# The scatter of a pair of experts' outputs, one token tile behind each step of the next pair's products, moved into groups of four tiles on four PSUM banks

## The chip, the core and the metric

One core of a Trainium2 chip runs the whole program in one launch. The metric is the device time of one execution in microseconds; the median of three runs is used. The engines are named as in the profile: PE is the matrix engine (its weight loads are listed apart as PEld), DVE, ACT and POOL are the vector, scalar and general engines, SP issues the weight loads, and the DMA engines carry them out.

## The reference, cut to what matters

The model has two layers. Each layer mixes tokens (an RG-LRU block in layer 0, an mLSTM in layer 1) and then applies a hierarchical mixture of experts. Layer 0 has 768 tokens (512 latent and 256 context), layer 1 has 512. For each token the mixture picks one of 4 groups and the best 2 of that group's 8 experts, 32 experts in all. The part that the change touches is this:

```
h2  = modulate(rms_norm(x, g2), sh2, sc2)
eid, wts = two experts of the best group, softmax of the two * p_group
f[token] = sum over its two experts of wts * ((silu(h2 @ w_gate[e]) * (h2 @ w_up[e])) @ w_down[e])
x   = x + gt2 * f
```

Everything is float32. An expert's three matrices are 1024x512, 1024x512 and 512x1024, so 6.29 MB; the 32 experts of a layer are 201.3 MB, and all of them are read once per layer.

## The kernel before, in words

Experts are worked on in 16 pairs per layer (index p, `moe`, the loop at line 1539). A pair has 128 slots, 64 per expert (96 and 32 for p = 5 to 10 of layer 0), and each slot holds one routed token. Per pair the program does, in this order:

- **Gate and up products** (`gate_up`, L1252): 16 steps. In a step the two experts of the pair each multiply one 128-row slice of their tokens with a 128x512 slice of a weight. Steps 0 to 3 use the first half of the gate matrices, 4 to 7 the first half of the up matrices, 8 to 11 and 12 to 15 the second halves. The sums gather in the PSUM tiles `pg` and `pu`. After each step, a table `fill` (step number to list of functions) says what else is put into the program there: loads of later weights, and the scatter of the pair before.
- **Transposes** of the next pair's gathered tokens (`tokens_T`, L1207) and of the hidden activations (`hidden_T`, L1268), and the look-up of a later pair's slots (L1165).
- **Down products** (`down`, L1277) in two column halves c = 0 and 1, into the PSUM tiles `pd`. DVE weighs each half with the gate (L1231, in layer 0 also L1235 and L1236), ACT rounds it to `yh` (L1239) and POOL forms the remainder `yl` (L1240).
- **Scatter** (`scatter_tile`, L1210 to L1215): the 128 slot rows go back to their tokens as a product with a one-hot table `oht`. For a token tile t (128 tokens) and a column half c this is two 128x512 matmuls on PE, one of `yh` and one of `yl`, into one PSUM bank (L1213), and one DVE addition of that bank to the token rows `x` in SBUF (L1215; the rows are named `xc` for context and `xl` for latent tokens). Layer 0 has 12 such (t, c) tiles per pair, layer 1 has 8. The list `todo` carries them to the next pair's `gate_up`; those of the last pair come after `rest()`, in turn on two `psc` and two `pdn` banks.

PSUM has eight banks here: two for `pg` and `pu`, two for `pd` (pool `pdn`), two for transposes (`ptr`), and two for the scatter (`psc`, tile name `ps`). The order of the work on PE, DVE, ACT, POOL and SP is that of the program text, since `manual_schedule` holds all five; a buffer is handed out again when its last reader is done, by semaphores.

Before the change, the pair's tiles stand one behind each of the last steps: steps 4 to 15 in layer 0, 8 to 15 in layer 1. In the last pair of a layer they stand in three groups behind steps 3, 7 and 11. All of them go through the two `psc` banks.

Weights come in pieces of 128 partitions x 8 KB (1.05 MB), 12 pieces (12.58 MB) per pair, through a ring of 15 buffers in layer 0 and 19 in layer 1 (`Ring`). SP issues them in program order (L93; the halves of the last pair's down matrices at L90), two behind every fourth step and four behind the down products; a load waits until the PE products that read its buffer are done.

Pair p = 5 of layer 0 (`extra`) has a second set of slots for its first expert: `more_up` runs behind steps 3, 7, 11 and 15 and keeps a `pdn` bank through the whole of `gate_up`; `more_scatter` follows behind step 3 of p = 6, after a one-hot table made on DVE (L1195).

Of the kernel before, what the change touches and what calls it, by code (L numbers as in the profile page):

```python
# [37 lines left out]
NPAIR = NE // 2  # L38
# [7 lines left out]
class Ring:  # L46
# [18 lines left out]
    def load(self, n, eng=None):  # L65
        for _ in range(n):
            if self.done < len(self.order):
                self.piece(*self.order[self.done], eng or self.net.nc.sync)
# [34 lines left out]
class Net:  # L103
# [994 lines left out]
    def moe(self, l, x, NT, ring, rt, tail):  # L1098
# [6 lines left out]
        with ExitStack() as st:  # L1105
# [21 lines left out]
            pdn = st.enter_context(tc.tile_pool(name="pdn", bufs=2, space=PSUM))  # L1127
            ptr = st.enter_context(tc.tile_pool(name="ptr", bufs=2, space=PSUM))
            psc = st.enter_context(tc.tile_pool(name="psc", bufs=2, space=PSUM))
# [61 lines left out]
            def onehot(oht, r):  # L1191

                rt_ = w1.tile([P, NT], F32, name="rt_")
                V.tensor_scalar(rt_, self.tile0[:, 0:NT], r, -1.0, op0=OP.subtract, op1=OP.mult)
                V.tensor_tensor(oht.rearrange("p (t n) -> p t n", n=P),  # L1195
                                self.iota1.unsqueeze(1).to_broadcast([P, NT, P]),
                                rt_.unsqueeze(2).to_broadcast([P, NT, P]), OP.is_equal)
# [5 lines left out]
            def tokens_T(xg, xT, n=P):  # L1203
                for h in range(2):
                    pt = ptr.tile([P, 4, P], F32, name="tr")
                    for j in range(4):
                        nc.tensor.transpose(pt[:, j, :], xg[:, h * 512 + j:h * 512 + 512:4], self.ident)  # L1207
                    nc.scalar.activation(xT[:, 4 * h:4 * h + 4, :], pt[:, :, 0:n], AF.Copy)  # L1208

            def scatter_tile(t, h, lhsT, ys, psum=None):  # L1210
                ps = (psum or psc).tile([P, 512], F32, name="pd" if psum is pdn else "ps")
                for i, y in enumerate(ys):
                    nc.tensor.matmul(ps, lhsT, y, start=i == 0, stop=i == len(ys) - 1)  # L1213
                xs = x[off + t][:, h * 512:(h + 1) * 512]
                V.tensor_add(xs, xs, ps)  # L1215

            def gates(r):

                g = w1.tile([P, D], F32, name="xg")
                V.tensor_scalar(g, gt[:, 0, :], r[:, 1:2], None, op0=OP.mult)  # L1220
                V.scalar_tensor_tensor(g, gt[:, 1, :], r[:, 2:3], g, op0=OP.mult, op1=OP.add)
                return g
# [19 lines left out]
            def gate_up(p, xT, fill):  # L1242

                e = (2 * p, 2 * p + 1)
                step = 0
                pg = pgu.tile([P, F], F32, name="pg")
                pu = pgu.tile([P, F], F32, name="pu")
                for h in range(2):
                    for n, ps in (("gate", pg), ("up", pu)):
                        for j in range(4):  # L1250
                            for a, w, i in cols(p):
                                nc.tensor.matmul(ps[a:a + w, :], xT[:, 4 * h + j, a:a + w],  # L1252
                                                 pieces[n, e[i], h][:, j, :], start=h == 0 and j == 0,
                                                 stop=h == 1 and j == 3)
                            for f in fill.pop(step, ()):
                                f()
                            step += 1
                s = w1.tile([P, F], F32, name="sg")
                nc.scalar.activation(s, pg, AF.Silu)  # L1259
                V.tensor_mul(s, s, pu)  # L1260
                return s

            def hidden_T(s):
                hT = w1.tile([P, 4, P], F32, name="hT")
                for h in range(2):
                    pt = ptr.tile([P, 4, P], F32, name="tr")[:, 0:2, :]
                    for j in range(2):
                        nc.tensor.transpose(pt[:, j, :], s[:, 256 * h + j:256 * h + 256:2], self.ident)  # L1268
                    nc.scalar.activation(hT[:, 2 * h:2 * h + 2, :], pt, AF.Copy)  # L1269
                return hT  # L1270
# [15 lines left out]
            extra = FIRST if l == 0 else None  # L1286
# [8 lines left out]
            def more_prep(p):  # L1295
                slots(p, table_more(p), rm, idm, P)
                gather(idm, xgm)

            def more_up(p, ps, h, c):

                if h == 0 and c == 0:
                    tokens_T(xgm, xTm, CAP)
                for j in range(4):
                    for a in range(2):
                        nc.tensor.matmul(ps[64 * a:64 * a + 64, 256 * c:256 * c + 256], xTm[:, 4 * h + j, :],
                                         pieces[("gate", "up")[c], 2 * p, h][:, j, 256 * a:256 * a + 256],
                                         start=h == 0 and c == 0 and j == 0,
                                         stop=h == 1 and c == 1 and j == 3, skip_group_check=True)
                if h == 1 and c == 1:
                    nc.scalar.activation(sm, ps[:, 0:256], AF.Silu)  # L1310
                    V.tensor_mul(sm, sm, ps[:, 256:512])
# [28 lines left out]
            def prepare(p):  # L1340

                rr[p] = wk.tile([P, 4], F32, name="slotr", bufs=4)
                idx = wk.tile([P, 1], I32, name="idx")
                oh = table(p)

                def step():
                    slots(p, oh, rr[p], idx, caps(p)[0])
                    xgs[p] = w1.tile([P, D], F32, name="xg")
                    gather(idx, xgs[p])
                return step  # L1350
# [187 lines left out]
            todo, nxt = [], None  # L1538
            for p in range(NPAIR):
                fill = {}  # L1540
                if p == 0:
                    fill = {1: [fill_ranks], 3: [fill_gather], 6: [fill_first]}
                    nxt = lambda: first[2]()
                for i, f in enumerate(todo):
                    at = 16 - len(todo) + i if p + 1 < NPAIR else 3 + 4 * (3 * i // len(todo))
                    fill.setdefault(at, []).append(lambda f=f: scatter_tile(*f))
                both = None
                if p + 1 == NPAIR:
                    if l == 0:
                        both = gates(rr[p])  # L1550
                    if begin:
                        begin(w1)

                for k in range(4):
                    fill.setdefault(4 * k + 3, []).append(lambda: load(2))
                if p == extra:
                    pm = pdn.tile([P, 512], F32, name="pd")
                    for k in range(4):
                        fill.setdefault(4 * k + 3, []).append(lambda k=k: more_up(extra, pm, k // 2, k % 2))
                elif p - 1 == extra:  # L1560
                    fill.setdefault(3, []).append(more_scatter)
                s = gate_up(p, xT, fill)
                if p + 1 < NPAIR:
                    xT = w1.tile([P, KD, P], F32, name="xT")
                    tokens_T(xgs[p + 1], xT)
                if nxt:
                    nxt()
                hT = hidden_T(s)
                nxt = prepare(p + 3) if p + 3 < NPAIR else None
                if p + 1 == extra:  # L1570
                    more_prep(extra)
                if p == extra:
                    more_down(p)
                oht = w1.tile([P, NT * P], F32R, name="oht")
                onehot(oht, rr[p][:, 0:1])
                yh = w1.tile([P, 2, 512], F32R, name="yh")
                yl = w1.tile([P, 2, 512], F32R, name="yl")
                for c in range(2):
                    down(p, hT, c, yh, yl, rr[p], both)
                load(4)  # L1580
                todo = [(t, c, oht[:, t * P:(t + 1) * P], (yh[:, c, :], yl[:, c, :]))
                        for c in range(2) for t in range(NT)]
# [587 lines left out]
```

## Time and profile before

| | |
|---|---|
| median of 3 runs | 1930.48 us (1927.62 to 1940.3) |
| the profiled execution | 1943.99 us, its span 1942.0 us |
| PE busy | 1799.0 us (93%) |
| PEld busy | 1009.0 us (52%) |
| DVE busy | 959.3 us (49%) |
| ACT busy | 542.7 us (28%) |
| POOL busy | 387.7 us (20%) |
| L1213, matmuls of yh (310) and yl (310) | 154.1 and 123.5 us |
| L1213, weight loads for yh (310) | 58.5 us |
| L1215, additions to xl (252) and xc (64) | 172.4 and 43.7 us |

The profile cuts the span into 40 slices of 48.55 us. The pairs of layer 0 lie in slices 10 to 21, those of layer 1 in slices 30 to 40. A matmul's listed duration overlaps that of the next one, so what a piece of work costs PE is read from the distance between starts, not from the durations.

### The profile page before, as it was taken

To read this page: it belongs to the slowest core of one execution; us is meant where nothing else is said; L and a number is where in the kernel's file an instruction comes from. 1 tells how busy PE (TensorE), PEld (TensorE's weight loads), DVE (VectorE), ACT (ScalarE), POOL (GpSimd) and SP (SyncE) were. 2 spreads that over 40 slices of the span, in tenths; PEclk is the share of its full clock that TensorE was granted. 3 is DMA by queue.
4 is the path that set the end of the run, shared out by engine and by line. 5 is a ranking of instruction groups with operands and counts; after the bars stand their busy time and mean duration, and the time that the engine had idled before them with its cause. 6 is when DMAs were issued, how large, how long until landed. Compare 5 with 4: busy or idle time off the path is not lost. (4 is left out here: it accounts for less than half of the span.)

```text
span 1942.0 us, 26118 instructions
## 1 busy us (share of the span) xinstructions
PE 1799.0 (93%) x10181; PEld 1009.0 (52%) x10181; DVE 959.3 (49%) x1879; ACT 542.7 (28%) x1007; POOL 387.7 (20%) x300
## 2 busy tenths in 40 slices
PE   7999988897999999999987998999978999999996
PEld 5777775683333333333336898976743333333332
DVE  5577767465454454444455743155552333233334
ACT  5367776222111101111115421145321111111112
POOL 3443311501101000101015242121211111110101
PEclk9999989898999999999998998999988999999998
DMA  9645432547999789999932544200869999999993
GB/s 326 186 142 163 152 109 76 188 152 311 420 419 397 278 326 409 389 403 389 400 117 76 176 139 155 85 1 17 311 257 400 421 421 420 421 422 421 421 420 135
DMA packets 158244, 527.75 MB, mean 272 GB/s; under 512 B 15132, under 2 KB 92194, under 8 KB 109988
## 3 DMA queue, kind: packets, MB, share of 16 engines
q1 hardware_dynamic: 151348, 497.09, 66.5%
q0 software_dynamic: 6768, 28.93, 3.8%
q8 instruction: 82, 1.34, 0.3%
q14 instruction: 46, 0.38, 0.1%
HBM read 518.59 MB, written 7.39 MB: 271 GB/s over the span
## 5 line engine op out<-in xcount | busy, mean ns | idle before, releaser
L1215 DVE TENSOR_TENSOR xl<-xl,ps 128x512 f32<-128x512 f32 x252 | 172.4, 687 | 335.6 <-PE ps L1213 335.6
L1213 PEld LDWEIGHTS ps<-yh,oht 128*128 128x128 f32 x310 | 58.5, 189 | 248.8 <-DVE xl L1215 129.0
L1213 PE MATMUL ps<-yh,oht 128*128 128x512 f32 x310 | 154.1, 497 | 8.9 <-DVEq L1356 6.1
L1200 POOL DMA_INDIRECT xg<-h_rows,idx x32 | 36.7, 1146 | 628.8 <-DVE slot L1185 263.1
L1277 PE MATMUL pd<-wring,hT 128*64 128x512 f32 (+1 forms) x616 | 152.4, 611 | 3.0 <-ACT hT L1269 2.6
L1252 PE MATMUL pu<-wring,xT 128*64 128x512 f32 (+1 forms) x576 | 154.1, 606 | 0.0
L309 POOL TENSOR_TENSOR wlo<-ws,whi 128x1024 fp32r<-128x1024 f32 x41 | 114.8, 2809 | 120.9 <-ACT whi L306 119.4
L1252 PE MATMUL pg<-wring,xT 128*64 128x512 f32 (+1 forms) x576 | 136.9, 601 | 0.0
L1240 POOL TENSOR_TENSOR yl<-yw,yh 128x512 fp32r<-128x512 f32 x60 | 76.6, 1277 | 255.5 <-ACT yh L1239 255.5
L1213 PE MATMUL ps<-yl,oht 128*128 128x512 f32 x310 | 123.5, 398 | 0.0
L1259 ACT ACTIVATE sg<-pg 128x512 f32<-128x512 f32 x32 | 19.1, 597 | 367.6 <-PE pg L1252 367.6
L1685 PE MATMUL pa<-whi,hhi 128*128 128x256 f32 x352 | 104.3, 296 | 9.1 <-ACT v L1782 9.0
L1239 ACT ACTIVATE yh<-yw 128x512 fp32r<-128x512 f32 x64 | 40.3, 630 | 251.7 <-DVE yw L1236 127.9
L1231 DVE SCALAR_TENSOR_TENSOR yw<-pd,slotr,gt2b 128x512 f32<-128x512 f32 x62 | 46.5, 751 | 118.9 <-PE pd L1277 118.9
L1685 PE MATMUL pa<-whi,hlo 128*128 128x256 f32 x352 | 103.3, 293 | 0.0
L1685 PE MATMUL pa<-wlo,hhi 128*128 128x256 f32 x352 | 102.9, 292 | 0.0
L1252 PE MATMUL pu<-yt,xT 128*64 128x512 f32 (+1 forms) x408 | 101.7, 605 | 0.0
L1208 ACT ACTIVATE xT<-tr 128x512 f32<-128x512 f32 x64 | 35.1, 596 | 221.0 <-PE tr L1207 221.0
L1277 PE MATMUL pd<-yt,hT 128*64 128x512 f32 (+1 forms) x376 | 87.6, 599 | 1.5 <-ACT hT L1269 1.0
L1252 PE MATMUL pg<-yt,xT 128*64 128x512 f32 (+1 forms) x400 | 84.7, 599 | 0.0
L1215 DVE TENSOR_TENSOR xc<-xc,ps 128x512 f32<-128x512 f32 x64 | 43.7, 687 | 82.1 <-PE ps L1213 82.0
L1277 PEld LDWEIGHTS pd<-wring,hT 128*64 128x64 f32 (+1 forms) x616 | 44.3, 133 | 75.7 <-issue 69.6
(627 smaller groups left out, 3727.9 us busy)
## 6 DMA issues: line engine op xcount, KB each, us to landing
wring<-in_l_moe_w_gate_dram SPq DMA_DIRECT2D x62, 1024.0 KB
wring<-in_l_moe_w_up_dram SPq DMA_DIRECT2D x61, 1024.0 KB
wring<-in_l_moe_w_down_dram SPq DMA_DIRECT2D x59, 1024.0 KB
yt<-in_l_moe_w_up_dram SPq DMA_DIRECT2D x41, 1024.0 KB
ws<-in_l_ada_w_dram SPq DMA_DIRECT2D x40, 1024.0 KB
yt<-in_l_moe_w_gate_dram SPq DMA_DIRECT2D x39, 1024.0 KB
yt<-in_l_moe_w_down_dram SPq DMA_DIRECT2D x35, 1024.0 KB
ws<-in_l_moe_w_gate_dram SPq DMA_DIRECT2D x24, 1024.0 KB
```

The costliest lines, as they stand in the source:

```text
L309: eng_lo.tensor_sub(lo, x, hi.bitcast(F32))
L1200: nc.gpsimd.indirect_dma_start(out=xg, out_offset=None, in_=hd, in_offset=bass.IndirectOffsetOnAxis(ap=idx[:, 0:1], axis=0))
L1208: nc.scalar.activation(xT[:, 4 * h:4 * h + 4, :], pt[:, :, 0:n], AF.Copy)
L1213: nc.tensor.matmul(ps, lhsT, y, start=i == 0, stop=i == len(ys) - 1)
L1215: V.tensor_add(xs, xs, ps)
L1231: V.scalar_tensor_tensor(y[k], ps, r[:, 1:2], g[:, 0, :], op0=OP.mult, op1=OP.mult)
L1239: nc.scalar.activation(yh, y, AF.Copy)
L1240: eng.tensor_sub(yl, y, yh.bitcast(F32))
L1252: nc.tensor.matmul(ps[a:a + w, :], xT[:, 4 * h + j, a:a + w], pieces[n, e[i], h][:, j, :], start=h == 0 and j == 0, stop=h == 1 and j == 3)
L1259: nc.scalar.activation(s, pg, AF.Silu)
L1277: nc.tensor.matmul(pd[a:a + w, :], hT[:, 2 * h + j, a:a + w], ring.down(2 * p + i, h, j, c), start=h == 0 and j == 0, stop=h == 1 and j == 1)
L1685: nc.tensor.matmul(ps, h, w[:, k % 4, :], start=k == 0 and j == 0, stop=k == KD - 1 and j == 2)
```

## The change

Only the table of steps in the loop over pairs is written anew, and the choice of PSUM banks for a scatter tile.

```
+                n = 2 if p == extra else 4
                 for i, f in enumerate(todo):
-                    at = 16 - len(todo) + i if p + 1 < NPAIR else 3 + 4 * (3 * i // len(todo))
-                    fill.setdefault(at, []).append(lambda f=f: scatter_tile(*f))
+                    g, k = divmod(i, n)
+                    at = 15 * (g + 1) * n // len(todo) - (3 if p + 1 < NPAIR else 2) + (n == 2)
+                    fill.setdefault(at, []).append(lambda f=f, k=k: scatter_tile(*f, psum=(psc, pdn)[k // 2]))
```

The tiles now stand in groups of four: behind steps 2, 7 and 12 in layer 0, and behind steps 4 and 12 in layer 1; in the last pair of a layer behind 3, 8 and 13, and 5 and 13. The first two tiles of a group use the `psc` banks, the last two the `pdn` banks that the down products use between. In pair p = 5 of layer 0, where `more_up` holds one `pdn` bank, there are six groups of two behind steps 0, 3, 5, 8, 10 and 13, on `psc` alone. No instruction is added or removed; on ACT, POOL and SP nothing moves.

On PE, pair p = 2 of layer 0 (`pg`, `pu`: gate and up products; `xT`: the tokens; `ps`, `pd`: the banks), first the place where the first tile stood:

```order
L1252 MATMUL pg<-wring,xT 64x512 x8
L1252 MATMUL pu<-wring,xT 64x512 x2
L1213 MATMUL ps<-yh,oht 128x512
L1213 MATMUL ps<-yl,oht 128x512
L1252 MATMUL pu<-wring,xT 64x512 x2
```

(two matmuls of L1252 are one step), and now the end of step 2, the first group and the start of step 3, with the buffers' numbers, which tell the banks apart:

```order
L1252 MATMUL pg_4089<-wring_3777,xT_3966 64x512
L1252 MATMUL pg_4089<-wring_3789,xT_3966 64x512
L1213 MATMUL ps_4097<-yh_4027,oht_4023 128x512
L1213 MATMUL ps_4097<-yl_4028,oht_4023 128x512
L1213 MATMUL ps_4101<-yh_4027,oht_4023 128x512
L1213 MATMUL ps_4101<-yl_4028,oht_4023 128x512
L1213 MATMUL pd_4105<-yh_4027,oht_4023 128x512
L1213 MATMUL pd_4105<-yl_4028,oht_4023 128x512
L1213 MATMUL pd_4109<-yh_4027,oht_4023 128x512
L1213 MATMUL pd_4109<-yl_4028,oht_4023 128x512
L1252 MATMUL pg_4089<-wring_3777,xT_3966 64x512
L1252 MATMUL pg_4089<-wring_3789,xT_3966 64x512
```

The first tile moves from behind step 4 to behind step 2, and eight scatter matmuls now follow each other with no product between them.

On DVE, the start of pair p = 6 of layer 0, after the extra pair (`yw`: the weighed outputs of p = 5; `xc`, `xl`: additions of scatter tiles; L1194 and L1195: the table of `more_scatter`):

```order
L1236 TENSOR_TENSOR yw_5327<-yw_5327,sg_5329 128x512
L1215 TENSOR_TENSOR xc_2780<-xc_2780,ps_5376 128x512
L1215 TENSOR_TENSOR xc_2780<-xc_2780,ps_5380 128x512
L1215 TENSOR_TENSOR xl_2776<-xl_2776,pd_5384 128x512
L1215 TENSOR_TENSOR xl_2776<-xl_2776,pd_5388 128x512
L1194 TENSOR_SCALAR rt__5401<-tile0_82,rm_3677 128x6
L1195 TENSOR_TENSOR sg_5400<-iota1_58,rt__5401 128x768
```

Before, L1194 and L1195 came right behind L1236; now the four additions of the first group stand ahead of them.

## Rows read from the trace of the kernel before

**Rows 1.** The page: GB/s moved by DMA in each of the 40 slices.

```profile
GB/s 326 186 142 163 152 109 76 188 152 311 420 419 397 278 326 409 389 403 389 400 117 76 176 139 155 85 1 17 311 257 400 421 421 420 421 422 421 421 420 135
```

**Rows 2.** Timeline of PE, layer 0, p = 2: start, duration, instruction, count, idle.

```profile
518.27 3.60 PE L1252 MATMUL pg<-wring,xT 128*64 128x512 f32 x16
521.70 1.03 PE L1252 MATMUL pu<-wring,xT 128*64 128x512 f32 x4
522.66 0.50 PE L1213 MATMUL ps<-yh,oht 128*128 128x512 f32 x1
522.99 0.40 PE L1213 MATMUL ps<-yl,oht 128*128 128x512 f32 x1
523.32 1.08 PE L1252 MATMUL pu<-wring,xT 128*64 128x512 f32 x4
...
541.61 1.11 PE L1207 MATMUL tr<-ident,xg 128*128 128x128 f32 x8
...
551.43 3.60 PE L1252 MATMUL pg<-yt,xT 128*64 128x512 f32 x16
```

**Rows 3.** Timeline of PE, last scatter of layer 0, on four banks.

```profile
1014.78 0.39 PE L1213 MATMUL ps<-yl,oht 128*128 128x512 f32 x1
1015.01 0.40 PE L1213 MATMUL pd<-yh,oht 128*128 128x512 f32 x1
1015.24 0.39 PE L1213 MATMUL pd<-yl,oht 128*128 128x512 f32 x1
```

**Rows 4.** Timeline of PE, last pair of layer 1: a group of two tiles, then the end.

```profile
1904.40 0.64 PE L1252 MATMUL pg<-yt,xT 128*64 128x512 f32 x1
...
1907.98 0.50 PE L1213 MATMUL ps<-yh,oht 128*128 128x512 f32 x1
...
1909.11 3.65 PE L1252 MATMUL pu<-wring,xT 128*64 128x512 f32 x16
...
1918.14 3.60 PE L1277 MATMUL pd<-ws,hT 128*64 128x512 f32 x16
```

**Rows 5.** Timeline of PE, last pair of layer 0: third tile of a group.

```profile
984.87 0.50 PE L1213 MATMUL ps<-yh,oht 128*128 128x512 f32 x1 [1.45 <-DVE xc L1215]
```

**Rows 6.** Timeline of POOL, layer 0: the remainder of p = 1, c = 0.

```profile
518.06 1.27 POOL L1240 TENSOR_TENSOR yl<-yw,yh 128x512 fp32r<-128x512 f32 x1 [5.28 <-ACT yh L1239]
```

**Rows 7.** Timeline of DVE, layer 0: last read of the pd banks; table of more_scatter.

```profile
519.25 0.74 DVE L1235 SCALAR_TENSOR_TENSOR sg<-pd,slotr,gt2b 128x512 f32<-128x512 f32 x1
...
677.08 0.96 DVE L1195 TENSOR_TENSOR sg<-iota,rt__5385 128x768 fp32r<-128x768 f32 x1
```

**Rows 8.** Timeline of PE, layer 0: the two longest waits, before p = 5 and in p = 6.

```profile
613.76 0.32 PE L1165 MATMUL tr<-tb,oh 128*128 128x2 bf16 x6 [3.02 <-DVE oh L1155]
...
678.18 0.73 PE L1213 MATMUL ps<-ym,sg 64*128 64x512 f32 x4 [2.04 <-DVE sg L1195]
```

**Rows 9.** Stretches: length, busy PE, PEld, DVE, ACT, POOL (instructions), PEclk, DMA share, GB/s.

```profile
614.00:620.00 6.00, 6.00 (x30) 2.01 (x28) 2.02 (x8) 0.18 (x1) 0.94 (x1) 0.50 1.01 412
...
1895.00:1900.00 5.00, 4.68 (x22) 1.77 (x20) 1.98 (x3) 0.00 (x0) 1.01 (x1) 1.00 1.05 386
...
1905.00:1906.00 1.00, 1.00 (x8) 0.31 (x6) 0.19 (x1) 0.00 (x0) 0.00 (x0) 1.00 0.44 178
...
1474.40:1895.00 420.60, 412.50 (x1904) 149.38 (x1902) 138.09 (x273) 53.32 (x112) 53.52 (x42) 1.00 1.01 420
747.10:978.70 231.60, 228.64 (x1326) 78.57 (x1319) 110.66 (x200) 26.85 (x55) 23.66 (x21) 1.00 0.98 395
```

**Rows 10.** DMA queues from 518.27 to 1003: SP's queue, packets, MB, share.

```profile
q1 hardware_dynamic: 26785, 170.28, 87.6%
```

**Rows 11.** DMA queues from 747.1 to 1003: SP's queue.

```profile
q1 hardware_dynamic: 15909, 91.13, 88.9%
```

**Rows 12.** DMA queues from 1474.4 to 1920: SP's queue.

```profile
q1 hardware_dynamic: 25491, 173.44, 93.8%
```

**Rows 13.** Waits, 1465 to 1900: PE's longest in total for a weight load.

```profile
PEld pu L1252 <- DMA wring<-in_l_moe_w_down_dram: 0.9, 3, 0.4
```

## The prediction

> **What bounds the kernel now.** I read the page's slices first, then the timeline of PE in one pair of each layer, then the DMA queues and stretches, then the timelines of DVE and POOL at the places where the change puts a new wait.
>
> The slices [rows 1] show two stretches in which DMA moves about 400 to 422 GB/s: slices 11 to 20 are the pairs of layer 0, slices 31 to 39 those of layer 1. In layer 1 DMA is full (share 1.01, 420 GB/s), and PE is busy for 412.50 of 420.60 us; in layer 0, from p = 8 on, it is 395 GB/s and 228.64 of 231.60 us [rows 9]. So both engines are nearly full, and the question for each layer is which would stop the other. Now it is PE: its longest wait for weights in layer 1 sums to 0.9 us [rows 13], and the third tile of a group in layer 0's last pair waited longer than that for a bank [rows 5].
>
> What PE does in a pair of layer 0 is read from starts [rows 2]. Four steps take 521.70 - 518.27 = 3.43 us, 0.86 each, so 16 take 13.7. The whole block, 518.27 to 541.61, takes 23.34. The remaining 9.6 us are its 12 scatter tiles, 0.80 each. A pair takes 551.43 - 518.27 = 33.16 us. In a tile yl starts 0.33 us behind yh and the next product 0.33 behind yl; the rest, some 0.15, is lost in going from products to scatter and back.
>
> **What the change does to the cost of a tile.** Where scatter matmuls follow each other and every bank is free, they start 0.23 us apart [rows 3]; those rows cross from one bank to the next, on the four banks that the groups will use. A group of two between products is in the trace too: the four steps from 1904.40 end 3.43 later, at 1907.83, and the next product starts at 1909.11 [rows 4], so two tiles cost 1.28 us. Four more matmuls at 0.23 make a group of four 2.2 us. Four single tiles cost 3.2. **A group saves 1.0 us.**
>
> **Layer 0.** Pairs 1 to 4 and 7 to 14 save three groups each: 12 x 3.0 = 36.0 us. Pair 5 has six groups of two, each 2 x 0.80 - 1.28 = 0.32 cheaper: 1.9. In pair 6 the four additions of the first group now stand on DVE ahead of the table of `more_scatter`, which started at 677.08 [rows 7] and for which PE already waits 2.04 us [rows 8]. Four additions at 0.69 (172.4 us over 252) put it off by 2.8, about what its first group will have saved, so I count the other two groups only: 2.0. The last pair had groups of four already, on two banks; I take back the one wait of 1.45 [rows 5] and leave its smaller ones at zero. Sum: 36.0 + 1.9 + 2.0 + 1.5 = **41 us**.
>
> The new waits are covered. The first group of p = 2 would start at 518.27 + 3 x 0.86 + 0.1 = 520.9. Its last input, yl of c = 0, is done at 518.06 + 1.27 = 519.3 [rows 6], and the last read of the `pd` banks ends at 519.25 + 0.74 = 520.0 [rows 7]; 1.6 and 0.9 us are left. Layer 1's first group stands two steps later. The additions of a group end some 3.5 us after its start (0.7 for the first tile, then 4 x 0.69), the products behind step 12 end at 2.2 + 3 x 0.86 = 4.8, so neither the multiplication of `sg` nor the next down products meet them. In pair 5 the group behind step 0 starts about when yl is done: nothing.
>
> Does DMA allow it? A pair needs 12.58 MB of weights and 0.52 MB of gathered rows, at 421 GB/s 31.1 us. PE's pair falls from 33.2 to 30.2, below that, so DMA's lead shrinks by 0.9 us a pair. From 518.27 SP's queue still brings 170.3 MB [rows 10], of which two pieces (2.1) belong to the next stage; 14 pairs need 176.2. So 8.0 MB lie ready, 19 us of DMA. Three pairs take 3 us of it, and slices 14 and 15 (278 and 326 GB/s, [rows 1]) show it filled again around p = 5 and 6. From 747.1, where p = 8 starts, 91.1 - 2.1 MB come [rows 11] and 100.7 are needed: 11.6 MB or 28 us ready, and eight pairs take 7. Layer 0 does not run dry.
>
> **Layer 1.** Two groups save 2.0 us a pair, 28 over 14 pairs, but here the saving runs into DMA. From 1474.4 to the end SP's queue brings 173.4 MB [rows 12] and POOL's 13 gathers of 0.52, at 420 GB/s 429 us: to 1904. The rate falls off at 1905 to 1906 [rows 9], so DMA ran full throughout and nothing that PE does lets it end before about 1905.5. Behind the last up piece come 4.19 MB of down weights and 0.52 MB of the final norm's row, at 386 GB/s [rows 9] 12.2 us: that piece lands near 1893.3. PE does its four steps and all behind them from 1909.11 to 1918.14 + 3.60 = 1921.74 [rows 4], 12.6 us, and the group behind step 13 adds 2.2: the products end at 1908.1. (The other limit, half of the last down half behind the last piece, is 1905.5 + 1.8 = 1907.3.) So layer 1 gains 1921.7 - 1908.1 = **13.6 us**, and PE waits for weights in its last pairs.
>
> **The sum.** 41 + 14 = 55 us off the profiled execution's 1944, so 1889. That execution is 13.5 us above the median of the runs, 1930.5, and I take the same 55 from that: **1876 us**.
>
> **Rivals.**
>
> - *A group's matmuls stay 0.33 us apart,* because each waits on its own bank's semaphore as single tiles do. For it: the third tile of a two-bank group. Against it: rows 3. A group then costs 8 x 0.33 + 0.15 = 2.8 and saves 0.4: 14 x 1.2 = 17 in layer 0, 14 x 0.8 = 11 in layer 1, where DMA then binds hardly. **1902**; 12%.
> - *No weight load overlaps a matmul within a group.* A load takes 0.19 us (58.5 us over 310), a matmul at most 0.23 [rows 3]; eight of both cost up to 3.4 against 3.2 now, so the time stays near **1930**. Against it: the same rows, where loads over all 128 rows keep the 0.23; 4%. The Trainium skill, "TensorE: Matmul & The Clock Gate", section "The mechanism", says that a load overlaps running matmuls only where its row group differs; by that the change would gain nothing, and the trace disagrees (0.23, where 0.42 would follow).
> - *PE's clock falls in layer 1* once PE waits for weights. A wait of 3.02 us [rows 8] was followed by a granted clock of 0.50, the 1.2 GHz level, for 6 us [rows 9]. If the last pairs end so, the 12.6 + 2.2 us behind the last up piece nearly double and layer 1 gains nothing: **1889**; 10%. The same page, section "A second HAM failure mode: psum-queue depth-cycling", has the clock go back and forth from short idle times between groups. Against it: the waits would be near 1.7 us (two pieces take DMA 5.2 us, PE 3.4), shorter than that one.
> - *DMA is not the limit in unprofiled runs.* The profiled one is 13.5 us slower, perhaps in DMA. Layer 1 then gains all 28: 1930.5 - 41 - 28 = **1861**; 10%.
> - *Slower: yl or a `pd` bank comes late in every first group.* PE is in order, so products, and with them the release of weights, queue behind it. It decides from about 3 us of wait on, because the clock then halves for some 6 us (3 us of work): 6 lost against 3 saved, 14 x 3 = 42, **1972**. It needs yl 4.6 us later than [rows 6] has it; 4%.
>
> **How the numbers follow.** The forecast has the other 60%. Its own range is 1868 to 1884 (0.05 us either way in a group's cost is 2 us in layer 0; half of layer 1's term). The range 1859 to 1903 takes in the second, third and fourth of the other cases that lie on the fast side and leaves out the two without a gain. About 1% is what a measurement of this kernel tells from no change. Faster by over 1% (below 1911): 60 + 12 + 10 + 10, less 2 for what I overlook, 90%; within 1%: 6%; slower: 4%.
>
> **What would show it.** Starts 0.23 us apart in groups, and 2.2 us from the last product of step 2 to the first of step 3; pairs of layer 0 of 30.2 us in place of 33.2; no wait of PE for DMA in layer 0; in layer 1 pairs of 28 us at first and 31 at the end, PE waiting for `wring` and `yt` pieces from about p = 9 on, DMA full up to the last piece and the last products about 3 us behind it. A wait on yl, or on DVE's read of `pd`, at the head of the groups would prove it wrong; so would 0.33 between their starts.

## The result, and the profile after

The changed kernel takes **1879.69 us** (median of four, 1873.74 to 1883.95) against 1935.28 (median of four, 1927.62 to 1940.3): a ratio of **0.973, interval 0.968 to 0.977**. In some executions of the kernel before, and of the variants below, the mean granted clock is lower (0.935 to 0.950, where the others have 0.954 to 0.967) and the time up to 2.6% longer; they are left out of all times and ratios here, and of the one profile among them ("last group behind step 15", 1911.5 us) only the two layers are read, since its extra time lies between them (454.0 us). The profiled execution took 1883.95 us (span 1881.9) against 1943.99 (1942.0).

To see where the 60 us went, I cut each profiled execution at the start of the first gate product and the start of the last down product of either layer:

| stretch, us | before | changed | difference | predicted |
|---|---|---|---|---|
| layer 0, first product to last | 554.7 | 514.8 | 39.9 | 41 |
| between the layers | 426.7 | 420.9 | 5.8 | 0 |
| layer 1, first product to last | 483.5 | 471.6 | 11.9 | 13.6 |
| from there to the end | 20.7 | 19.1 | 1.6 | 0 |

(0.8 us more lie ahead of layer 0.) The two layers, which the change touches, gave 51.8. The other 8 come from work that it does not touch; in eleven of the twelve other profiles of this study, which have that work unchanged, the stretch between the layers takes 410.6 to 422.4 us, so the profiled execution of before was a long one there. A second profile of the changed kernel gave 512.4 and 470.5 us for the layers, 418.7 between them and 20.3 from there to the end.

The page, GB/s of DMA in 40 slices, answers to [rows 1]; a slice is 47.05 us now:

```profile
GB/s 331 176 156 150 127 122 91 179 173 233 418 419 419 386 323 419 419 419 418 418 165 83 164 157 179 46 1 39 301 277 398 422 421 420 421 421 420 421 421 246
```

Slices 16 to 20, the later pairs of layer 0, are full now (418 to 419, where 389 to 409 stood). The timeline of PE of p = 2, layer 0, answers to [rows 2] (start, duration, engine, line, operation, tiles, shape, count):

```profile
514.61 2.75 PE L1252 MATMUL pg<-wring,xT 128*64 128x512 f32 x12
517.28 0.50 PE L1213 MATMUL ps<-yh,oht 128*128 128x512 f32 x1
517.62 0.40 PE L1213 MATMUL ps<-yl,oht 128*128 128x512 f32 x1
517.86 0.39 PE L1213 MATMUL ps<-yh,oht 128*128 128x512 f32 x1
518.09 0.40 PE L1213 MATMUL ps<-yl,oht 128*128 128x512 f32 x1
518.33 0.39 PE L1213 MATMUL pd<-yh,oht 128*128 128x512 f32 x1
...
519.35 1.08 PE L1252 MATMUL pg<-wring,xT 128*64 128x512 f32 x4
...
532.35 2.79 PE L1252 MATMUL pu<-ws,xT 128*64 128x512 f32 x12
535.07 1.23 PE L1207 MATMUL tr<-ident,xg 128*128 128x128 f32 x8
...
545.01 1.46 PE L1252 MATMUL pg<-yt,xT 128*64 128x512 f32 x6
```

Only the first yl is 0.34 us behind its yh; from there the starts are 0.23 apart, across the change of banks too. Three steps from 514.61 end at 517.18 (0.86 each), so the group takes 519.35 - 517.18 = 2.17 us. The block is 20.46 us long (23.34 before), the pair 30.40 (33.16 before). The input of the group is early, as POOL's timeline shows, against [rows 6]: 514.40 + 1.27 = 515.67, where 517.3 was wanted.

```profile
514.40 1.27 POOL L1240 TENSOR_TENSOR yl<-yw,yh 128x512 fp32r<-128x512 f32 x1 [5.28 <-ACT yh L1239]
```

The third tile of a group in the last pair of layer 0, which waited 1.45 us in [rows 5], waits for nothing:

```profile
952.34 0.40 PE L1213 MATMUL pd<-yh,oht 128*128 128x512 f32 x1
```

Pair by pair, from one pair's first gate product to the next one's:

| us a pair | before | changed |
|---|---|---|
| layer 0, p = 1 to 3, and 7 to 13 | 33.0 to 33.2 | 30.3 to 30.5 |
| p = 4; p = 14 | 39.6; 32.9 | 36.7; 29.9 |
| p = 5; p = 6 | 48.3; 41.6 | 44.7; 41.8 |
| p = 15, to its last down product | 32.2 | 28.9 |
| layer 1, p = 1 to 10 | 29.9 | 28.2 |
| p = 11, 12, 13, 14 | 29.9, 29.9, 29.9, 29.7 | 30.7, 31.2, 31.1, 30.7 |
| p = 15, to its last down product | 28.2 | 29.0 |

In layer 1, pairs of 28.2 us run until p = 10, and then pairs of about 31, DMA's time for a pair. The list of waits from 1420 to 1870 us (line, what is waited for: us in total, times, longest), against [rows 13], and one such wait in PE's timeline:

```profile
PEld pu L1252 <- DMA wring<-in_l_moe_w_up_dram: 7.4, 9, 1.9
PE pu L1252 <- DMA wring<-in_l_moe_w_up_dram: 2.0, 2, 1.0
PE pu L1252 <- DMA ws<-in_l_moe_w_up_dram: 1.6, 2, 1.0
```

```profile
1777.35 1.07 PE L1252 MATMUL pu<-wring,xT 128*64 128x512 f32 x2 [0.94 <-DMA wring<-in_l_moe_w_up_dram]
```

Stretches, as in [rows 9] (length, busy PE, PEld, DVE, ACT, POOL, granted clock, DMA share, GB/s):

```profile
1480.00:1835.00 355.00, 344.78 (x1648) 141.21 (x1646) 113.49 (x234) 46.03 (x97) 46.69 (x36) 1.00 1.01 421
1859.00:1860.00 1.00, 1.00 (x8) 0.30 (x6) 0.00 (x0) 0.00 (x0) 0.00 (x0) 1.00 0.27 111
747.00:930.00 183.00, 180.81 (x1141) 76.27 (x1135) 92.77 (x181) 23.24 (x48) 21.15 (x18) 1.00 1.01 418
```

DMA is full throughout layer 1 and PE's granted clock stays 1.00, its 2.4 GHz level, in spite of the waits. The last row shows DMA full in layer 0 as well. The end of layer 1, against [rows 4]:

```profile
1859.73 3.60 PE L1277 MATMUL pd<-ws,hT 128*64 128x512 f32 x16
```

### The profile page after: what moved, and what is told of

The parts are those of the page before. It is cut to its first block, busy times and chain, and to the rows that moved or that the text cites. A ratio compares the mean times of both kernels' runs of the same rounds, so it can differ in the third digit from the quotient of the medians.

```text
span 1881.9 us, 26126 instructions
## 1 busy us (share of the span) xinstructions
PE 1742.4 (93%) x10181; PEld 1041.3 (55%) x10181; DVE 948.0 (50%) x1879; ACT 543.5 (29%) x1007; POOL 384.1 (20%) x300
## 5 line engine op out<-in xcount | busy, mean ns | idle before, releaser
L1215 DVE TENSOR_TENSOR xl<-xl,ps 128x512 f32<-128x512 f32 x136 | 87.7, 683 | 302.4 <-PE ps L1213 302.4
L1200 POOL DMA_INDIRECT xg<-h_rows,idx x32 | 36.7, 1146 | 582.7 <-DVE slot L1185 249.1
L1252 PE MATMUL pu<-wring,xT 128*64 128x512 f32 (+1 forms) x576 | 149.9, 610 | 2.0 <-DMA wring<-in_l_moe_w_up_dram 2.0
L1252 PE MATMUL pg<-wring,xT 128*64 128x512 f32 (+1 forms) x576 | 127.7, 594 | 0.0
L1259 ACT ACTIVATE sg<-pg 128x512 f32<-128x512 f32 x32 | 19.1, 597 | 355.3 <-PE pg L1252 355.3
L1252 PE MATMUL pu<-yt,xT 128*64 128x512 f32 (+1 forms) x408 | 95.6, 596 | 0.3 <-DMA yt<-in_l_moe_w_up_dram 0.3
L1252 PEld LDWEIGHTS pu<-wring,xT 128*64 128x64 f32 (+1 forms) x576 | 40.9, 132 | 76.7 <-issue 68.5
L1215 DVE TENSOR_TENSOR xl<-xl,pd 128x512 f32<-128x512 f32 x128 | 82.1, 680 | 0.5 <-PE pd L1213 0.5
L1252 PE MATMUL pg<-yt,xT 128*64 128x512 f32 (+1 forms) x400 | 81.4, 596 | 0.0
L1213 PE MATMUL ps<-yh,oht 128*128 128x512 f32 x166 | 75.4, 454 | 5.9 <-DVEq L1356 5.9
L1252 PEld LDWEIGHTS pg<-wring,xT 128*64 128x64 f32 (+1 forms) x576 | 38.5, 131 | 70.9 <-issue 68.6
```

The source lines that it names most:

```text
L1200: nc.gpsimd.indirect_dma_start(out=xg, out_offset=None, in_=hd, in_offset=bass.IndirectOffsetOnAxis(ap=idx[:, 0:1], axis=0))
```

## The experiments

The theory: PE pays for each change between the products and the scatter, layer 0 gets the whole saving, and layer 1 what DMA leaves of it. The rivals: the banks alone, the place alone, something other than DMA in layer 1. In the experiments, "layer 0" and "layer 1" followed by a time are the two stretches of the table above. Three profiles with layer 0 as before give 554.4 to 555.0 us there; five with layer 0 as changed 512.4 to 514.8.

**Four banks without groups.**

```
-  fill.setdefault(at, []).append(lambda f=f: scatter_tile(*f))
+  fill.setdefault(at, []).append(lambda f=f, b=i % 4 // 2 if p != extra else 0:
+                                 scatter_tile(*f, psum=(psc, pdn)[b]))
```

> One tile behind a step as before, but the tiles take the two psc and the two pdn banks in turn (pair p = 5 of layer 0 stays on psc). Theory (the gain of 55 us is the number of changes between products and scatter on PE, so of the tiles' grouping): a single tile still costs 0.80 us, 1935 us (1928 to 1940). Rival 'banks' (a single tile waits for its bank until DVE has added the one before the last; twice as many banks take that wait away): a tile falls to 0.55 us (2 x 0.23 and the 0.1 between), and the time to the 1880 us of the changed kernel.

Measured: 1929.4 us, ratio to before 0.999 (0.994 to 1.003); layer 0 552.1 us, layer 1 482.6. PE's timeline, p = 2:

```profile
524.43 1.08 PE L1252 MATMUL pu<-wring,xT 128*64 128x512 f32 x4
525.44 0.50 PE L1213 MATMUL pd<-yh,oht 128*128 128x512 f32 x1
525.78 0.39 PE L1213 MATMUL pd<-yl,oht 128*128 128x512 f32 x1
526.10 1.08 PE L1252 MATMUL pu<-wring,xT 128*64 128x512 f32 x4
```

A step and a tile take 526.10 - 524.43 = 1.67 us on a `pd` bank that has been free for long: still 0.81 for the tile, yl still 0.34 behind. The rival "banks" is false, and the 0.33 is a price of changing over, not a wait. Ordinary pairs take 33.0 to 33.2 us as before. Only the last pairs fall, from 32.2 to 29.0 us in layer 0 and from 28.2 to 27.1 in layer 1: their tiles stood in groups already, and there the banks are all that was missing.

**Groups of four on two banks.**

```
-  ... lambda f=f, k=k: scatter_tile(*f, psum=(psc, pdn)[k // 2])
+  ... lambda f=f: scatter_tile(*f)
```

> Groups of four as in the changed kernel, at the same steps, but all on the two psc banks. Theory: a group of four on two banks is in the last pair of the kernel before, its second group: 2.86 us there, with 0.41 us of wait for DVE at the third tile, against 2.2 on four banks and 3.2 for four single tiles. So a good third of the gain is left: 14 x 3 x 0.34 + 4 = 18 us in layer 0 and 14 x 2 x 0.34 = 10 in layer 1, 1907 us (1898 to 1916). If the grouping alone were everything and the banks nothing: 1880. If the banks were everything: 1935.

Measured: 1918.6 and 1919.1 us, two executions only; layer 0 541.3 us, layer 1 478.0. So 13 and 5 us less than before, where I had expected 18 and 10: some of a gain is left, about 0.2 us a group in layer 0, less than the 0.34 that I worked out. PE's timeline, p = 2:

```profile
518.70 0.40 PE L1213 MATMUL ps<-yl,oht 128*128 128x512 f32 x1
519.41 0.50 PE L1213 MATMUL ps<-yh,oht 128*128 128x512 f32 x1 [0.31 <-DVE xc L1215]
519.75 0.40 PE L1213 MATMUL ps<-yl,oht 128*128 128x512 f32 x1
```

The third tile starts 0.71 us behind the second one's yl in place of 0.23, and its yl is 0.34 behind again. A group needs both halves of the change: four tiles together, and four banks for them.

**Single tiles two steps earlier.**

```
-  at = 16 - len(todo) + i if p + 1 < NPAIR else ...
+  at = 14 - len(todo) + i if p + 1 < NPAIR else ...
```

> One tile behind a step on the two psc banks as before, only two steps earlier (behind steps 2 to 13 of layer 0 and 6 to 13 of layer 1; the last pairs as before). Theory: a tile costs the same 0.80 us anywhere, 1935 us (1928 to 1940). Rival 'place' (the gain comes from the tiles' standing earlier, because the last additions held up what follows step 15): most of the gain, about 1890 us.

Measured: six times from 1932.8 to 1955.5 us, ratio 1.008 (1.002 to 1.014), so slower than before by 0.8%; layer 0 560.8 us, layer 1 487.3. An ordinary pair takes 0.33 us more in layer 0 and 0.35 more in layer 1 (30.3 for 29.9). I had not expected a loss. The end of the block shows its cause:

```profile
536.49 1.94 PE L1252 MATMUL pu<-ws,xT 128*64 128x512 f32 x8
538.36 1.23 PE L1207 MATMUL tr<-ident,xg 128*128 128x128 f32 x8
```

Two steps end at 538.21, and the transposes start at 538.36. They take 1.23 us here, and 1.11 in [rows 2], where a scatter tile stood ahead of them. In the kernel before, the last tile of a pair led straight into the transposes and so had no way back to products to pay for; moved forward, it has one. So the place does matter, in the direction against the change: the changed kernel loses the same at the end of each pair and gains in spite of it.

**The change in one layer alone.** An `if l == 1` (or 0) that sets `at` as before and `k` to 0.

> The change in layer 0 alone; layer 1 keeps single tiles on psc. Theory: layer 0 gives 41 us whatever layer 1 does, so 1894 us (1888 to 1900). If instead the two layers share something (weights of layer 1 that come early, or a clock that stays up), it is off that by 5 us or more; the profile of the changed kernel has 5.7 us between the layers that the change does not explain.

> The change in layer 1 alone; layer 0 keeps single tiles on psc. Theory: layer 1 gives 12 to 14 us, so 1921 us, and in the profile the stretch from layer 1's first product to its last down product is 471.6 us as in the changed kernel (483.5 before), with PE waiting for weights in the last pairs. Rival 'not DMA' (the cap of the changed kernel's layer 1 came from something that layer 0's change left behind): all of 24 to 28 us, 458 us for the stretch, 1908 us.

Measured for layer 0 alone: 1890.0 us, ratio 0.978 (0.971 to 0.986), stretches 514.7 and 482.5. For layer 1 alone: eight times, median 1918.6, ratio 0.995 (0.991 to 0.998), stretches 554.4 and 470.5. Each layer has its stretch of the changed kernel, whatever the other does, and the stretch between them is 422.2 and 410.6: the 5.8 us there belong to neither layer's change.

**Less for DMA to bring in layer 1,** in the kernel before and in the changed one:

```
-  for i in range(2):                                      # down pieces
+  for i in range(2 if l == 0 or p + 1 == NPAIR else 1):
...
+  if l == 1 and name == "down" and e < 2 * NPAIR - 2:
+      self.pieces[name, e + 1, h] = w
...
-  load(4)
+  load(4 if l == 0 else 2)
```

> The kernel before, but in layer 1 the second expert of pairs 0 to 14 uses the first one's down weights, so 10 of 12 pieces are loaded per pair (the output is another one); the instructions on PE, DVE, ACT and POOL are as many as before. A pair then needs 10.49 + 0.52 MB, at 421 GB/s 26.1 us instead of 31.1. Theory: before the change layer 1 was bound by PE, so the stretch of layer 1 stays 482 to 484 us, and the time 1931 to 1935. Rival 'DMA bound already': the stretch shrinks by 5 us or more.

> The changed kernel with the same two pieces per pair left out in layer 1 (the output is another one). Theory: DMA no longer caps layer 1, so the gain of its groups doubles: 0.86 to 1.0 us a group, 24 to 28 us for the stretch of layer 1, which falls to 456 to 460 us (471.6 in the changed kernel), and the time to about 1867 us. PE's waits for weights in layer 1 go, and the pair period is 28.5 to 29 us to the end. Rival 'not DMA': the stretch stays 470 us or more, since what a group saves in layer 1 is less than in layer 0.

Measured with single tiles: ratio 1.001 (0.998 to 1.005), layer 1 482.7 us: the kernel before was not bound by DMA. With groups: 1865.6 to 1880.3 us, ratio 0.971 (0.965 to 0.977), layer 1 **456.9** us. All pairs from p = 1 to 13 take 28.2 us, and PE's list of waits has none for weights:

```profile
1480.00:1820.00 340.00, 333.39 (x1632) 138.05 (x1630) 112.78 (x233) 45.87 (x96) 45.42 (x35) 1.00 0.97 379
```

So PE's saving in layer 1 is 482.7 - 456.9 = 25.8 us, and DMA leaves 12 of it. That is shown in the profiled executions. As the four times scattered, I ran it again:

> The same kernel as light_groups (two pieces per pair left out in layer 1; the output is another one), for more times: its four lie between 1865.6 and 1880.3. Theory (DMA caps layer 1 of the changed kernel in executions without the profiler too): the median lies 10 to 15 us below the 1879.5 of the changed kernel, 1865 to 1870, and about 0.966 of the kernel before. Rival (d) of the prediction (without the profiler DMA was no limit, so fewer pieces give nothing): 1877 to 1882, 0.973. The stretch of layer 1 in the profile: 457 us.

Measured: five times, median 1868.8 us, ratio 0.968 (0.965 to 0.971), layer 1 457.8. Over all of them the light kernel's nine times have a mean of 1870.3 and the changed kernel's ten one of 1879.7. Without the two profiled executions of each kernel the means are 1871.1 and 1879.2. So DMA is the cap in executions that are not profiled as well; the 8 to 9 us there are fewer than the 13 to 14 of the profiles, and with the light kernel's times spread over 17 us that difference is not settled.

**How far grouping goes,** beside the changed kernel as it is:

```
groups of six:
-  n = 2 if p == extra else 4
+  n = 2 if p == extra else 6 if l == 0 else 4
-  ... scatter_tile(*f, psum=(psc, pdn)[k // 2])
+  ... scatter_tile(*f, psum=(psc, pdn)[k % 4 // 2])
last group behind step 15:
+  if l == 0 and n == 4 and p + 1 < NPAIR:
+      at += 3
eight, then four (with g, k = divmod(i, 8) under the first condition; banks as in groups of six):
+  if l == 0 and n == 4 and p + 1 < NPAIR:
+      at = (6, 15)[g]
+  elif l == 1 and p + 1 == NPAIR:
+      at = (4, 9)[g]
```

> The changed kernel unaltered, as the measure for the three beside it. All theories: 1880 us (1875 to 1885); the stretch of layer 0 from its first product to its last down product 514.7 us, that of layer 1 471 us, and what lies between them anything from 410 to 427.

> Layer 0's tiles in two groups of six behind steps 4 and 12 (last pair 5 and 13) on the four banks in turn (psc, psc, pdn, pdn, psc, psc); all else as changed. Theory (what counts is how often PE goes over): one change to scatter and back less per pair, which is 0.80 - 0.47 = 0.33 us (0.47 for each further tile), so 4 us: 510.5 us for the stretch of layer 0, if DVE's additions (0.69 each) free the first bank before the fifth tile wants it, which it does 1.4 us behind the group's start against 1.84. Rival 'banks decide': the fifth and sixth tile wait, and the stretch stays 514 us or grows.

> Layer 0's groups of four behind steps 5, 10 and 15 in place of 2, 7 and 12 (pair 5 and the last pair as changed). Theory: behind step 15 come the transposes, not products, so one of the ways back to products goes; tiles two steps earlier lost 6 us in layer 0 by the opposite move (560.8 against 554), 0.4 us a pair. So 4 to 6 us: 509 to 511 us for the stretch of layer 0. Rival 'DVE in the way': the four additions end 3.5 us behind the group's start and hold up the multiplication of sg and the down products' pd banks, some 0.5 to 1 us a pair: 517 us or more.

> Layer 0: eight tiles behind step 6 and four behind step 15; the last pair of layer 1 has its two groups behind steps 4 and 9 in place of 5 and 13. Theory: both savings of layer 0 together, less a wait of 0.25 to 0.5 us at the eighth tile: 506 to 509 us for the stretch of layer 0. The scatter that stood behind the last up piece of layer 1 (2.2 us) is then done while PE waits for that piece: 1 to 2 us off the stretch of layer 1. In all 6 to 10 us below the changed kernel, 1872 us. Rival 'DMA caps layer 0 too': the lead of 12 us at the end of layer 0 runs out, PE waits for weights in its last pairs, and the stretch stays at 511 us or more.

| | us, median | ratio to before | layer 0 | layer 1 |
|---|---|---|---|---|
| the changed kernel again | 1879.5 | 0.974 (0.970 to 0.977) | 512.4 | 470.5 |
| groups of six | 1876.0 | 0.971 (0.966 to 0.975) | 508.2 | 471.4 |
| last group behind step 15 | 1873.5 | 0.971 (0.967 to 0.975) | 509.8 | 470.9 |
| eight, then four | 1873.4 | 0.971 (0.967 to 0.974) | 505.5 | 470.7 |

The stretches of layer 0 hold pairs 4 and 6, which differ from profile to profile in the same code (pair 4 of the changed kernel's layer 0 takes 35.4 to 36.9 us), so the savings are better read from the eleven ordinary pairs without pair 4, which repeat to 0.02 us in all. There groups of six save 0.33 us a pair, as expected; the last group behind step 15 saves 0.18, half of the 0.4 expected; eight, then four saves 0.48, nearly both together (a pair takes 29.9 us for 30.4). With a group behind step 15 the rival "DVE in the way" is true in a small part: its additions put off the multiplication of `sg`, and the down products start 1.51 us behind the look-up in place of 1.37 (p = 2). **It is faster than both kernels**: its five times, 1871.1 to 1875.4, all lie below the six of the changed kernel on the same chip, 1876.8 to 1884.4. Its timeline, p = 2:

```profile
523.97 0.39 PE L1213 MATMUL pd<-yh,oht 128*128 128x512 f32 x1
524.20 0.40 PE L1213 MATMUL pd<-yl,oht 128*128 128x512 f32 x1
524.44 0.43 PE L1213 MATMUL pd<-yh,oht 128*128 128x512 f32 x1
...
534.64 0.40 PE L1213 MATMUL pd<-yl,oht 128*128 128x512 f32 x1
534.88 1.12 PE L1207 MATMUL tr<-ident,xg 128*128 128x128 f32 x8
```

The eighth tile keeps the 0.23 (I had expected it to wait 0.25 to 0.5), since DVE's additions follow each other faster than their listed 0.69 us: pairs of them start 1.20 us apart (521.84, 523.04, 524.24), so a bank comes free every 0.60. The transposes start 0.24 behind the last yl and take 1.12.

The part about layer 1 does not show in the stretch, which at 470.7 us is no shorter than the changed kernel's second one. But the first pair of layer 1, which has no scatter, took 37.1 us in this profile, against 36.9 and 35.7 in the two of the changed kernel. The last pair took 28.0 us to its last down product, against 29.0 and 29.2, and the wait of 0.7 us for the last up piece, in the first profile of the changed kernel, is gone: about 1 us, the lower end of what was expected, from one profile. DMA did not stop layer 0: PE's list of waits there has none for a weight.

## Why the prediction was right

The forecast was 1876 us, the time 1879.7; what it stood on is what the trace shows. That layer 0 as a whole came out so near (39.9 us for 41) is in part luck: four terms are off, by -2.9, +1.7, +1.8 and -2.2 us, and nearly cancel, and two of the four are the granted clock and not the scatter.

- **The price of a tile and of a group**: right. 2.17 us for 2.2, starts 0.23 us apart, no wait for yl or a bank in ordinary pairs. The first rival (0.33 within a group, 1902 us) is false by the timeline. So is the second: a group has eight loads over all 128 rows, each listed at 0.19 us, and its eight matmuls still start 0.23 us apart behind the first. The Trainium skill, "TensorE: Matmul & The Clock Gate", section "The mechanism", says in one place that a load overlaps running matmuls only where its row group differs, which this trace contradicts, and in another that a load into the background weight buffer is pulled ahead of them too, which would allow it; whether that buffer is at work here, no run shows.
- **Twelve ordinary pairs of layer 0**: 36.0 predicted, 33.1 measured (2.76 a pair; in the second profile 34.4, pair 4 having taken 35.4 us). The working priced all 12 tiles of a pair at 0.80, as an average, and so overlooked that the last one led into the transposes. Some 0.24 us a pair go there: the tiles moved two steps earlier lost 0.33 by it, and the group behind step 15 got 0.18 back. In layer 1 the same makes 1.7 us a pair of 2.0.
- **Pair 15 of layer 0**: 1.5 predicted, 3.3 measured. All of it comes from the banks (29.0 us with four banks alone): I had taken back only the longest wait and set the smaller ones, and the wider spacing behind each, to zero.
- **Pair 5**: 1.9 predicted, 3.6 measured. The groups gave what was predicted: from its first product to the transposes of the next tokens the pair took 32.2 us before and takes 30.3 now. The other 1.7 us lie behind them, in the down products of the second set of slots (L1322), which took 665.64 - 660.36 = 5.28 us before and take 649.91 - 646.33 = 3.58 now, behind the same wait. PE's timeline, before and after:

```profile
660.36 3.04 PE L1322 MATMUL ps<-yt,xgm 128*64 128x512 f32 x8 [0.47 <-ACT xgm L1317]
```

```profile
646.33 1.94 PE L1322 MATMUL ps<-yt,xgm 128*64 128x512 f32 x8 [0.47 <-ACT xgm L1317]
```

  The granted clock there was 0.50 from 662 to 664 us before, and is 1.00 now. In the five profiles with single tiles in layer 0 the pair takes 48.2 to 48.4 us, in the nine with groups 44.7; why the clock stays up with groups is not shown.
- **Pair 6**: 2.0 predicted, and it lost 0.2 (it gained 0.7 in the second profile). DVE's table came late, as foreseen, but two things were not. The first group met a late yl, the wait that the prediction had called covered everywhere; and after these waits PE's clock fell. PE's timeline and the stretches:

```profile
660.67 0.50 PE L1213 MATMUL ps<-yl,oht 128*128 128x512 f32 x1 [0.68 <-POOL yl L1240]
...
664.87 0.73 PE L1213 MATMUL ps<-ym,sg 64*128 64x512 f32 x4 [1.31 <-DVE sg L1195]
```

```profile
668.00:672.00 4.00, 4.00 (x16) 2.28 (x18) 4.00 (x8) 0.00 (x0) 0.00 (x0) 0.66 1.00 420
672.00:676.00 4.00, 4.00 (x23) 0.81 (x19) 0.90 (x2) 0.00 (x0) 0.00 (x0) 0.50 0.08 33
```

  The wait for the table, 1.31 us, is shorter than the 2.04 of [rows 8], but with the 0.68 for yl there is about as much waiting in all. Then comes a stretch at 0.50, the 1.2 GHz level: products that start 0.43 us apart elsewhere start 0.85 apart from 671.71 to 675.98, which is 2.1 us lost, the size of the missing term. But this fall is no price of the change alone: two other profiles with single tiles in layer 0 have the wait of 2.04 us as well, the granted clock falls behind it there too (to 0.74 and 0.50 from 683 to 687 us in the kernel before with fewer loads in layer 1), and the pair takes 43.1 us. The profiled execution of before, with 41.6, was one that kept its clock. Against 43.1 the two profiles of the changed kernel gain 1.3 and 2.3 us, so the 2.0 is not shown to be wrong.
- **Layer 1 is capped by DMA**: right, and shown by the experiment with fewer pieces. 13.6 us predicted, 11.9 measured, 13.0 in the second profile; the two differ in the first pair alone, which has no scatter, and without it either gives 12.0. Pairs of 28 us first and 31 then, as said; the change between them came at p = 11, not at 9. That a pair saved 1.7 us and not 2.0 explains about one pair of the two, by an estimate: ten pairs of 28.2 us use up the lead that nine of 27.9 would (31.1 us less the pair, each); the other is left open. The last products end at 1863.3; DMA's rate is 293 GB/s from 1856 to 1858 and 154 in the two microseconds after, so they end some 5 us behind its fall, where 2.6 had been worked out.
- **The clock in layer 1** (third rival, 1889 us): false. The waits are 1 to 1.9 us, and the clock stays 1.00.
- **DMA not the limit without the profiler** (fourth, 1861): false. With fewer pieces the times are 9 us lower, so at 1879.7 the changed kernel is limited.
- **Slower** (1972): its wait occurs once, in p = 6, and not in every pair.
- **From the profiled execution to the median**: I took the same 55 us off both. That holds for the layers (51.8), and the other 8 us by which the profiled executions differ lie in untouched work.
- **The range**: the sentence on it counts the rivals wrongly; 1859 to 1903 takes in the first, third and fourth of the list.

## What to carry to other kernels

Price a step that is moved by what stands ahead of it and behind it, at the place that it leaves too: here a scatter tile cost 0.80 us between products, 0.47 for each further one in a group, and less where it led into transposes. An idle time in front of an instruction can look like a wait for a buffer and be a price of order; twice as many banks alone gained nothing in ordinary pairs, the grouping needed them all the same. And before a saving is added up over a stage, work out how far the other full engine is from its own limit: in layer 1 half of PE's gain was DMA's to refuse, while layer 0 got all of it from weights that lay ready.

## What the runs showed of the hardware that was not expected

- Waits of about 2 us in p = 6 of layer 0 are followed by a lower clock in some executions and not in others. One wait of 2.04 us in the kernel before left it at 1.00, and one of 2.03 in "eight, then four" did too; the same 2.04 with fewer loads in layer 1 was followed by 0.74 and 0.50 over 4 us, one of 2.03 with groups of six by 0.57 over 4 us, the 0.68 and 1.31 of the changed kernel by 0.66 and 0.50. Nothing here tells what decides.
- The stretch between the layers, with the same instructions, took from 410.6 to 426.7 us in thirteen of the fourteen profiles, a spread of 0.8% of the whole time. Stretches of the two layers repeat to 3 us, and eleven ordinary pairs of layer 0 to 0.02 us in all, so small changes are better read from them than from the total.
- The same eight transposes take 1.23 us behind products (128x64 tiles in f32) and 1.11 behind scatter matmuls.
